# Delta net's merges: the 64 by 64 products of two heads staggered instead of all eight at once

## The chip, the cores and the metric

The kernel runs on one core of a Trainium2 chip. The metric is the device time of one execution in microseconds (us); the time of a kernel is the median of its runs. Before the change that is 2497.89 us, the median of three runs from 2497.13 to 2501.19 us.

Engines are named as the profile names them: PE is TensorE's matmul and PEld its weight load, DVE is VectorE, ACT is ScalarE, POOL is GpSimd and SP is the engine that issues most of the DMAs.

## The reference, cut to what matters

The program is a small streaming encoder on 1024 tokens of width 1024: one gated DeltaNet layer with a gated ConvFFN, then one chunked attention layer with another ConvFFN, then a norm. The change lies in the DeltaNet layer. There, for each of 8 heads and each chunk, a unit lower triangular matrix is solved against the values and the keys:

```python
m = jnp.where(strict, jnp.einsum("bhnid,bhnjd->bhnij", k_beta, k) * decay, 0.0)
eye = jnp.eye(CHUNK, dtype=m.dtype)
rhs = jnp.concatenate([v * beta[..., None], k_beta * jnp.exp(gcum)[..., None]], axis=-1)
uw = lax.linalg.triangular_solve(m + eye, rhs, left_side=True, lower=True, unit_diagonal=True)
```

After it a scan over the chunks carries a 128 by 128 state per head.

## The kernel before, in words

**The stage.** The kernel works on chunks of 128 tokens, so there are 8 chunks, and each of the 8 heads has a 128 by 128 triangular matrix per chunk. Heads and chunks are cut in four groups `t`: group `t` holds four heads (0 to 3 or 4 to 7) and four chunks (`s`, the first or the second half of the sequence). For each group the steps are: `gram` (products of keys, one matrix `mn` per chunk), `invert_blocks` (inverts the 16 by 16 blocks on the diagonal), `merge` twice (`j` = 0, 1; each for two heads with four chunks each, so eight matrices), `prep`, `chain` (the scan, per head four chunks of small fp32 matmuls at lines 926, 930 and 939), `output` and `finish`. That makes eight merges.

**A merge** puts the inverse `U` of a 128 by 128 matrix together from the inverted blocks: first 16 by 16 blocks into 32 by 32 (lines 845 and 851), then those into 64 by 64 (lines 862, 872 and 874), then those into 128 by 128. The last doubling has two products of 64 by 64 for each of the eight matrices. The lower half, line 881, reads rows 0 to 63 of `mn` and of `TY` and writes rows 64 to 127 of `pm`, a tile in PSUM. ACT copies that into `TY[64:128]` (line 883). The corner, line 886, reads rows 64 to 127 of `TY` and of `U` and writes rows 0 to 63 of `pm`, and ACT copies it into `U` (line 888). `pm` is one tile of 128 rows by 8 matrices by 64 columns, with one buffer, and all the products of a merge write into it, lines 845 to 874 too. Products in fp32 are run as two passes, so eight products are 16 matmul instructions in the trace.

**What sets the order.** While these small steps run, PE works through the dense projections: matmuls of 128 by 128 weights with 512 columns, three per step (lines 118, 119 and 120, split precision; `acc` for the input projections, `acco` for the output projection). The order of PE's, DVE's and ACT's instructions is written out when the program is built, by a planner, the class `Flow`. It keeps a clock `T` of PE and a free time for each other engine. Each step of the small work is a generator that says what it costs (`wv.pe(n, dt)` moves `T`, `wv.on("A", cost)` books time on ACT) and yields the time at which its results should be there; `run` takes the first small step whose time has come (plus a slack of 0.5), and else one dense step. A step's `wv.mark(("merged", hd, s), t)` lets that head's `chain` start; the marks of all heads let the output projection start, through `begin`. So a step that is cut in two, or another cost or yield, moves other steps in the program as well, though it adds no instruction to them.

Of the kernel before, what the change touches and what calls it, by code (L numbers as in the profile page):

```python
# [28 lines left out]
def trunk_kernel(  # L29
# [15 lines left out]
    nc = tc.nc  # L45
# [32 lines left out]
    mm = nc.tensor.matmul  # L78
# [321 lines left out]
    wv = None  # L400
# [107 lines left out]
    with ExitStack() as ph:  # L508
# [137 lines left out]
        def heads(t):  # L646

            return t // 2, range(4 * (t % 2), 4 * (t % 2) + 4)
# [172 lines left out]
        TY = dq.tile([P, 8, 64], F32, name="TY")  # L821
        nc.gpsimd.memset(TY, 0.0)

        def merge(t, j):

            b = [slice(32 * i, 32 * i + 32) for i in range(4)]
            D = dq.tile([P, 8, 32], F32, name="D", tag="D", bufs=1)
            s, hds = heads(t)
            hds = hds[2 * j : 2 * j + 2]
            for a in range(2):  # L830
                nc.sync.dma_start(out=D[:, 4 * a : 4 * a + 4], in_=d_us[t][2 * j + a].rearrange("c b j i -> (b j) c i"))
            U = dp.tile([P, 8, P], F32, name="U", tag="U", bufs=2)
            nc.gpsimd.memset(U, 0.0)
            wv.on("G", 0.83)
            yield wv.T + 4.5 - wv.slack
            T = dq.tile([P, 8, 32], F32, name="T", tag="T", bufs=1)
            X = dq.tile([P, 8, 32], F32, name="X", tag="X", bufs=1)
            pm = pone.tile([P, 8, 64], F32, name="pm", tag="pm")
            blocks = [(a, c, 4 * a + c) for a in range(2) for c in range(4)]
            mn = [mns[hd, s] for hd in hds]  # L840
            nc.vector.transpose(T.rearrange("p c i -> p (c i)"), D.rearrange("p c i -> p (c i)"))
            yield wv.on("D", 0.5)
            for a, c, n in blocks:
                for i in range(4):
                    mm(pm[b[i], n, 0:32], mn[a][b[i], c, b[i]], T[b[i], n], start=True, stop=True)
            wv.pe(32, 0.03)
            nc.scalar.copy(X, pm[:, :, 0:32])
            yield wv.on("A", 0.39)
            for a, c, n in blocks:
                for i in range(4):  # L850
                    mm(pm[b[i], n, 32:64], X[b[i], n], D[b[i], n], start=True, stop=True)
            wv.pe(32, 0.03)
            nc.vector.scalar_tensor_tensor(D[:, :, 16:32], pm[:, :, 48:64], upper, D[:, :, 16:32], op0=ALU.mult, op1=ALU.add)
            nc.vector.transpose(T.rearrange("p c i -> p (c i)"), D.rearrange("p c i -> p (c i)"))
            t_ = wv.on("D", 0.85)
            for i in range(4):
                nc.gpsimd.tensor_copy(U[b[i], :, b[i]], D[b[i]])
            wv.on("G", 1.37, t_)
            yield t_
            for a, c, n in blocks:  # L860
                for i in (0, 2):
                    mm(pm[b[i + 1], n, 0:32], mn[a][b[i], c, b[i + 1]], T[b[i], n], start=True, stop=True)
            wv.pe(16, 0.04)
            for i in (1, 3):
                nc.scalar.copy(X[b[i]], pm[b[i], :, 0:32])
            t_ = wv.on("A", 0.74)
            for i in (0, 1):
                nc.scalar.copy(TY[b[i], :, b[i]], T[b[i]])
            wv.on("A", 0.8)
            yield t_  # L870
            for a, c, n in blocks:
                mm(pm[b[1], n, 32:64], D[b[1], n], X[b[1], n], start=True, stop=True)
                for i in (0, 2):
                    mm(pm[b[i], n, 32:64], X[b[i + 1], n], D[b[i + 1], n], start=True, stop=True)
            wv.pe(24, 0.04)
            nc.scalar.copy(TY[b[1], :, 0:32], pm[b[1], :, 32:64])
            for i in (0, 2):
                nc.vector.tensor_copy(U[b[i], :, b[i + 1]], pm[b[i], :, 32:64])
            yield max(wv.on("D", 0.8), wv.on("A", 0.4))
            for a, c, n in blocks:  # L880
                mm(pm[64:128, n], mn[a][0:64, c, 64:128], TY[0:64, n], start=True, stop=True)
            wv.pe(8, 0.12)
            nc.scalar.copy(TY[64:128], pm[64:128])
            yield wv.on("A", 0.6)
            for a, c, n in blocks:
                mm(pm[0:64, n], TY[64:128, n], U[64:128, n, 64:128], start=True, stop=True)
            wv.pe(8, 0.12)
            nc.scalar.copy(U[0:64, :, 64:128], pm[0:64])
            t_ = wv.on("A", 0.6)
            for a, hd in enumerate(hds):  # L890
                Us[hd, s] = U[:, 4 * a : 4 * a + 4]
                wv.mark(("merged", hd, s), t_)

        outs = [-1, -1]
        states = dp.tile([P, 8, P], F32, name="states")
# [339 lines left out]
        kqs, mns, parts, Us = {}, {}, {}, {}  # L1235
# [94 lines left out]
        wv = Flow()  # L1330
# [20 lines left out]
        with tc.manual_schedule(engines={mybir.EngineType.PE, mybir.EngineType.DVE, mybir.EngineType.Activation}):  # L1351
# [4 lines left out]
            for t in range(4):  # L1356
                s, hds = heads(t)
                for hd in hds:
                    wv.add(2, "sq", wv.when(("q", hd, 0) if s == 0 else ("in", hd)), qnorm(hd, s))
                    if s == 1:  # L1360
                        wv.add(1, "fetch", wv.when(("out", hd, 0), ("k", hd, 1), ("q", hd, 1)), fetch_kq(hd))
                wv.add(2, "gram", wv.when("gates"), gram(t))
                wv.add(2, "solve", wv.when(*[("gram", hd, s) for hd in hds]), invert_blocks(t))
                for j in range(2):
                    free = [("chain", t - 1, j)] if t > 0 else []
                    for hd in hds[2 * j : 2 * j + 2]:
                        wv.add(3, "prep", wv.when(("v", hd, s), ("qn", hd, s), ("scale", t), ("gram", hd, s), *free), prep(hd, s))
                        wv.add(0, ("chain", hd % 2), lambda: 0.0, chain(t, hd))
                    wv.add(1, "merge", wv.when(("solved", t), *free), merge(t, j))
                    wv.add(2.5, ("joined", t, j), lambda: 0.0, joined(t, j))  # L1370
                    wv.add(2, "finish", wv.when(("chain", t, j), *[("qn", hd, s) for hd in hds]), finish(t, j))
# [725 lines left out]
    with ExitStack() as ph:  # L2097
# [17 lines left out]
        wv = Flow()  # L2115
# [300 lines left out]
        def close(p, a, tp, oT, t):  # L2416
            if p == 7 and a == 1 and tp % 2 == 1:
                wv.add(1, ("own", tp // 2), wv.when(("acts", tp // 2)), own_act(oT, tp // 2, 7))
            if p < 7 and (a, tp) == (1, 3):
                if p == 6:  # L2420
                    for s in range(2):
                        wv.add(2, ("own", s), wv.when(("acts", s)), own_act(oT, s, 6))
                wv.mark(("o", p), t)
                if p < 6:
                    wv.later(t + 5.0, lambda: (nc.sync.dma_start(out=d_o[p], in_=oT), wv.mark(("d_o", p), wv.T + 5.31)))

        def own_act(oT, s, k):
            split_act(acts, oT[:, hs(s)], s, k)
            t = wv.on("A", 0.31)
            wv.mark(("act", k, s), wv.on("D", 1.09, t) if k % 2 == 0 else wv.on("G", 2.22, t))  # L2430
            return
            yield
# [291 lines left out]
```

## Time and profile before

| what | value |
|---|---|
| runs | 2497.13, 2497.89, 2501.19 us; median 2497.89 |
| profiled execution, first to last instruction (its own time) | 2493.3 us |
| PE busy | 2466.1 us, 99%, 13785 matmuls |
| DVE, ACT, POOL busy | 1842.5, 1442.1, 1523.0 us (74%, 58%, 61%) |
| TensorE clock granted | 9 tenths or more in every slice |
| merges | from 152.3 us (first product of the first) to about 541 us (last product of the eighth) |

A row of the profile that names a line stands for all instructions of that line on one engine: their count, the time in which at least one ran, the mean duration of one, and the idle time of the engine ahead of them with what ended it. Matmuls overlap: a dense matmul of 512 columns shows a duration of about 390 ns though the next starts 230 ns later. So what a piece of PE's work costs is read from starts, from the first instruction of the piece to the first one behind it.

### The profile page before, as it was taken

What the parts mean: (1) busy time and instruction counts of PE and PEld (TensorE: products, weight loads), DVE (VectorE), ACT (ScalarE), POOL (GpSimd) and SP (SyncE); (2) the same over time, 40 slices, a digit from 0 to 9 for tenths busy, and PEclk for the clock granted to TensorE, in tenths of its full rate; (3) what the DMA queues carried; (4) which work ended last, traced back from release to release, by engine and by line L of the source; (5) the groups of instructions that cost most, each with busy time, mean ns of one, the idle gap of its engine ahead of it and who ended that gap; (6) DMA issues with size and microseconds to landing.
All of it is one profiled execution on the core that took longest, in us unless ns stands there. A gap on an engine that the chain in (4) does not pass through costs nothing.

```text
span 2493.3 us, 39279 instructions
## 1 busy us (share of the span) xinstructions
PE 2466.1 (99%) x13785; PEld 2057.0 (83%) x13785; DVE 1842.5 (74%) x2985; ACT 1442.1 (58%) x2770; POOL 1523.0 (61%) x1548
## 2 busy tenths in 40 slices
PE   8999999999999999999999999999999999999998
PEld 6888888888888888888788888888877888888877
DVE  5665874567798888888866656666589788888886
ACT  6444546474465556565555666667456565666555
POOL 3655653357357777777626454455554777778774
PEclk9999999999999999999999999999999999999999
DMA  8734435565347777777841232333444799777788
GB/s 228 188 105 118 142 110 153 156 194 163 96 108 148 150 153 151 153 144 156 183 151 55 67 80 77 81 76 95 145 114 119 184 176 180 166 169 171 152 187 224
DMA packets 383877, 353.19 MB, mean 142 GB/s; under 512 B 97600, under 2 KB 304448, under 8 KB 383680
## 3 DMA queue, kind: packets, MB, share of 16 engines
q1 hardware_dynamic: 350704, 243.46, 34.4%
q0 software_dynamic: 28224, 98.58, 22.5%
q10 hardware_dynamic: 4752, 8.65, 0.9%
q8 instruction: 108, 1.77, 0.3%
q14 instruction: 89, 0.73, 0.1%
HBM read 182.25 MB, written 156.30 MB: 136 GB/s over the span
## 4 chain that ended last, share of the span: by engine, by line
PE 81%; POOL 6%; DVE 4%; issue 4%; DMA 2%; ACT 2%; SPq 0%; ACTq 0%; POOLq 0%; DVEq 0%
PE acc L118 8%; PE pu L1448 8%; PE acc L119 8%; PE acc L120 8%; PE pu L1446 8%; PE pu L1447 8%; PE pd L1448 3%; PE pd L1446 3%; PE pd L1447 3%; POOL ul L1412 3%; PE acco L118 2%; PE acco L120 2%; PE acco L119 2%; PE ptp L2353 2%; PE poT L2399 1%
## 5 line engine op out<-in xcount | busy, mean ns | idle before, releaser
L1412 POOL TENSOR_TENSOR ul<-r,uh 128x512 fp32r<-128x512 f32 x266 | 430.4, 1638 | 258.3 <-ACT uh L1434 253.5
L118 PE MATMUL acc<-xh,whi 128*128 128x512 f32 x896 | 369.3, 413 | 0.5 <-ACT xh L1094 0.5
L119 PE MATMUL acc<-xl,whi 128*128 128x512 f32 x896 | 352.1, 393 | 0.4 <-POOL xl L381 0.3
L120 PE MATMUL acc<-xh,wlo 128*128 128x512 f32 x896 | 351.3, 392 | 0.0
L103 POOL TENSOR_TENSOR wlo<-wraw,whi 128x256 fp32r<-128x256 f32 (+1 forms) x326 | 237.0, 758 | 107.8 <-ACT whi L101 105.3
L1434 ACT CAST uh<-r 128x512 fp32r<-128x512 f32 x289 | 177.1, 623 | 183.3 <-DVE r L1412 148.8
L1448 PE MATMUL pu<-xh,ul 128*128 128x512 f32 x524 | 204.4, 390 | 0.7 <-POOL ul L1412 0.7
L1446 PE MATMUL pu<-xh,uh 128*128 128x512 f32 x524 | 204.4, 390 | 0.7 <-ACT keep L1575 0.7
L1802 ACT COPY stage<-pd 128x1024 f32<-128x1024 f32 x180 | 175.3, 1014 | 49.7 <-PE pd L1448 48.8
L1447 PE MATMUL pu<-xl,uh 128*128 128x512 f32 x524 | 203.9, 389 | 0.0
L120 PEld LDWEIGHTS acc<-xh,wlo 128*128 128x128 f32 x896 | 168.5, 188 | 37.1
L2308 POOL TENSOR_SCALAR sS<-sS,st 128x640 f32<-128x640 f32 (+4 forms) x128 | 87.6, 691 | 178.4 <-DVE st L2306 168.2
L119 PEld LDWEIGHTS acc<-xl,whi 128*128 128x128 f32 x896 | 169.3, 189 | 28.4 <-POOL xl L381 2.5
L118 PEld LDWEIGHTS acc<-xh,whi 128*128 128x128 f32 x896 | 169.1, 189 | 27.5 <-ACT xh L1094 0.9
L1412 POOL TENSOR_TENSOR dl<-a,dh 128x512 fp32r<-128x512 f32 x90 | 153.3, 1703 | 47.4 <-ACT dh L1434 37.2
L1541 DVE SCALAR_TENSOR_TENSOR gate<-gpre,colt,gate 128x1023 f32<-128x1023 f32 (+2 forms) x92 | 176.5, 1919 | 2.5 <-ACT gate L1538 1.8
L1541 DVE SCALAR_TENSOR_TENSOR val<-vpre,colt,val 128x1023 f32<-128x1023 f32 x88 | 149.2, 1696 | 29.3 <-ACT val L1538 29.3
L2298 DVE CUSTOM_DVE_ANT_0 sS<-sc,bt 128x640 f32<-128x640 f32 (+4 forms) x128 | 84.1, 657 | 111.4 <-PE sc L2294 75.9
L1412 DVE TENSOR_TENSOR r<-r,r 128x512 f32<-128x512 f32 x160 | 130.3, 814 | 32.8 <-POOL ul L1412 31.7
L1412 DVE TENSOR_TENSOR el<-val,eh 128x512 fp32r<-128x512 f32 x90 | 85.4, 949 | 43.2 <-ACT eh L1434 43.2
L1448 PEld LDWEIGHTS pu<-xh,ul 128*128 128x128 f32 x524 | 98.4, 188 | 22.8 <-POOL ul L1412 1.4
L1446 PEld LDWEIGHTS pu<-xh,uh 128*128 128x128 f32 x524 | 98.4, 188 | 21.1 <-ACT keep L1575 1.1
(428 smaller groups left out, 7197.9 us busy)
## 6 DMA issues: line engine op xcount, KB each, us to landing
r<-in_f_w_up_dram SPq DMA_DIRECT2D x176, 256.0 KB, 4.5
d_r<-stage POOLq DMA_DIRECT2D x78, 512.0 KB, 8.1
d_c<-stage POOLq DMA_DIRECT2D x70, 512.0 KB, 8.4
a<-in_f_w_down_dram SPq DMA_DIRECT2D x72, 256.0 KB, 2.9
wraw<-in_a_w_in_dram SPq DMA_DIRECT2D x32, 512.0 KB, 4.5
d_e<-stage POOLq DMA_DIRECT2D x32, 512.0 KB, 8.3
wraw<-in_a_w_out_dram SPq DMA_DIRECT2D x16, 512.0 KB, 4.1
d_r<-h ACTq DMA_DIRECT2D x32, 256.0 KB, 2.8
```

Of the source, the lines that this page charges most:

```text
L103: nc.gpsimd.tensor_tensor(lo[:, c], raw[:, c], hi[:, c].bitcast(F32), op=ALU.subtract)
L118: mm(ps, hi[:, kw, wcol : wcol + P], rh[k][s], start=st, stop=False)
L119: mm(ps, hi[:, kw, wcol : wcol + P], rl[k][s], start=False, stop=False)
L120: mm(ps, lo[:, kw, wcol : wcol + P], rh[k][s], start=False, stop=sp)
L1412: tt = lambda eng, o, a, b, op: eng.tensor_tensor(o, a, b, op=op)
L1434: copy(hi, src)
L1446: mm(ps, w[0][:, cw], x[0], start=first, stop=False, skip_group_check=True)
L1447: mm(ps, w[0][:, cw], x[1], start=False, stop=False, skip_group_check=True)
L1448: mm(ps, w[1][:, cw], x[0], start=False, stop=last, skip_group_check=True)
L1541: nc.vector.scalar_tensor_tensor(t_[:, a:c1], p_[:, a - step : c1 - step], w[:, 2 - step : 3 - step], t_[:, a:c1], op0=ALU.mult, op1=ALU.add)
L1802: nc.scalar.copy(t_, ps)
L2308: nc.gpsimd.tensor_scalar(S, S, st[:, 3:4], 1.0, op0=ALU.mult, op1=ALU.mult)
```

## The change

The eight lower halves and the eight corners of a merge are no longer two blocks of eight. The four lower halves of the first head run alone. Then the four corners of the first head run in turns with the four lower halves of the second head. Then the four corners of the second head run alone. The copies of ACT are cut by head: two into `TY` and two into `U` in place of one each. The first head is marked as merged after the middle block, the second after the last. The planner is told other costs (`wv.pe(4, 0.12)`, `wv.pe(4, 0.14)`, `wv.pe(4, 0.12)` and four copies of 0.4 in place of two of 0.6), and there is one more yield.

```diff
-            for a, c, n in blocks:
-                mm(pm[64:128, n], mn[a][0:64, c, 64:128], TY[0:64, n], start=True, stop=True)
-            wv.pe(8, 0.12)
-            nc.scalar.copy(TY[64:128], pm[64:128])
-            yield wv.on("A", 0.6)
-            for a, c, n in blocks:
-                mm(pm[0:64, n], TY[64:128, n], U[64:128, n, 64:128], start=True, stop=True)
-            wv.pe(8, 0.12)
-            nc.scalar.copy(U[0:64, :, 64:128], pm[0:64])
-            t_ = wv.on("A", 0.6)
-            for a, hd in enumerate(hds):
-                Us[hd, s] = U[:, 4 * a : 4 * a + 4]
-                wv.mark(("merged", hd, s), t_)
+            def low(a, c):
+                mm(pm[64:128, 4 * a + c], mn[a][0:64, c, 64:128], TY[0:64, 4 * a + c], start=True, stop=True)
+
+            def corner(a, c):
+                mm(pm[0:64, 4 * a + c], TY[64:128, 4 * a + c], U[64:128, 4 * a + c, 64:128], start=True, stop=True)
+
+            def close(a):
+                nc.scalar.copy(U[0:64, 4 * a : 4 * a + 4, 64:128], pm[0:64, 4 * a : 4 * a + 4])
+                Us[hds[a], s] = U[:, 4 * a : 4 * a + 4]
+                wv.mark(("merged", hds[a], s), wv.on("A", 0.4))
+
+            for c in range(4):
+                low(0, c)
+            wv.pe(4, 0.12)
+            nc.scalar.copy(TY[64:128, 0:4], pm[64:128, 0:4])
+            yield wv.on("A", 0.4)
+            for c in range(4):
+                corner(0, c)
+                low(1, c)
+            wv.pe(4, 0.14)
+            nc.scalar.copy(TY[64:128, 4:8], pm[64:128, 4:8])
+            t_ = wv.on("A", 0.4)
+            close(0)
+            yield t_
+            for c in range(4):
+                corner(1, c)
+            wv.pe(4, 0.12)
+            close(1)
```

In the changed kernel the lower half keeps line 881, the corner is line 884, the copies are lines 894 and 900 (`TY`) and 887 (`U`), and every later line stands 15 further down. The number of instructions is the same on PE, DVE, POOL and SP; ACT has 16 copies more.

On PE, in the first merge, before the change (`pk` are transposes for `prep`, `acc` is the dense work):

```order
L881 MATMUL pm<-TY,mn 64x64 x8
L750 MATMUL pk<-ident,kq 128x128 x4
L118 MATMUL acc<-xh_0_247,whi 128x512
L119 MATMUL acc<-xl_0_248,whi 128x512
L120 MATMUL acc<-xh_0_247,wlo 128x512
L118 MATMUL acc<-xh_0_251,whi 128x512
L119 MATMUL acc<-xl_0_252,whi 128x512
L120 MATMUL acc<-xh_0_251,wlo 128x512
L886 MATMUL pm<-U,TY 64x64 x8
```

The same place of PE after the change:

```order
L881 MATMUL pm<-TY,mn 64x64 x4
L750 MATMUL pk<-ident,kq 128x128 x4
L118 MATMUL acc<-xh_0_247,whi 128x512
L119 MATMUL acc<-xl_0_248,whi 128x512
L120 MATMUL acc<-xh_0_247,wlo 128x512
L118 MATMUL acc<-xh_0_251,whi 128x512
L119 MATMUL acc<-xl_0_252,whi 128x512
L120 MATMUL acc<-xh_0_251,wlo 128x512
L884 MATMUL pm<-U,TY 64x64
L881 MATMUL pm<-TY,mn 64x64
L884 MATMUL pm<-U,TY 64x64
L881 MATMUL pm<-TY,mn 64x64
```

The block of lower halves has become four, and the block of corners a mix of four and four (the rest of it goes on in the same way); the last four corners come as a third block after four more dense steps.

On ACT, at the same merge, before the change, from the copy into `TY` to the one into `U`:

```order
L883 COPY TY<-pm 64x512
L754 ACTIVATE ke<-pk,ekd 128x128 x4
L625 ACTIVATE th<-u 128x512
L101 CAST whi<-wraw 128x1024
L888 COPY U<-pm 64x8x64
```

And after the change:

```order
L894 COPY TY<-pm 64x256
L754 ACTIVATE ke<-pk,ekd 128x128 x4
L101 CAST whi<-wraw 128x1024
L625 ACTIVATE th<-u 128x512
L900 COPY TY<-pm 64x256
L887 COPY U<-pm 64x4x64
```

The copy that the last four corners wait for, line 900, stands behind the same four `ke`, one cast of weights and one `th`.

On PE, at the end of the eighth merge, where the dense work of the input projections runs out and the output projection (`acco`) begins, before the change (`pc` is the chain):

```order
L886 MATMUL pm<-U,TY 64x64 x8
L118 MATMUL acc<-xh_1_261,whi 128x512
L119 MATMUL acc<-xl_1_262,whi 128x512
L120 MATMUL acc<-xh_1_261,wlo 128x512
L930 MATMUL pc<-vv,U 128x128 x2
L118 MATMUL acco<-xh_0_6121,whi 128x512
```

And after the change (`pv` are transposes for `prep`; lines 941 and 945 are what lines 926 and 930 were):

```order
L118 MATMUL acc<-xh_1_261,whi 128x512
L119 MATMUL acc<-xl_1_262,whi 128x512
L120 MATMUL acc<-xh_1_261,wlo 128x512
L945 MATMUL pc<-vv,U 128x128
L941 MATMUL pc<-states,kq 128x128
L884 MATMUL pm<-U,TY 64x64 x4
L778 MATMUL pv<-ident,vv 128x128 x4
L945 MATMUL pc<-vv,U 128x128
L118 MATMUL acco<-xh_0_6146,whi 128x512
```

The last block of corners now stands behind the last dense step of the input projections, and between that step and the first one of the output projection there are five pieces of small work instead of one.

## The prediction, on record before the result

> **What bounds the kernel now.** I read the page first, for the engine that has no room.
>
> ```profile
> span 2493.3 us, 39279 instructions
> PE 2466.1 (99%) x13785; PEld 2057.0 (83%) x13785; DVE 1842.5 (74%) x2985; ACT 1442.1 (58%) x2770; POOL 1523.0 (61%) x1548
> ```
>
> PE is busy for 99% of the span. That is an average over very different stages, so next comes the stretch in which the eight merges lie, by the view of windows and by the view of waits with PE as the one that waits.
>
> ```profile
> 150.00:550.00 400.00, 399.56 (x3948) 340.19 (x3947) 244.13 (x689) 219.70 (x637) 198.89 (x268) 1.00 0.48 142
> PE po L985 <- DVE mn L724: 0.2, 1, 0.2
> PE pv L778 <- DMA vv<-d_v: 0.2, 1, 0.2
> ```
>
> The columns of the first line are the stretch, its length, and the busy time of PE, PEld, DVE, ACT and POOL; then the clock and the DMA share. Of 400 us PE has 399.56 busy, and it waited twice, 0.2 us each, neither time in a merge. DVE, ACT and POOL have at least 155 us free each. So in this stage a microsecond is won only by giving PE less to do, or lost by giving it more or by making it wait. What the groups of lines say of the two products and of the copies behind them is the same:
>
> ```profile
> L881 PE MATMUL pm<-TY,mn 64*64 64x64 f32 x128 | 9.1, 221 | 0.0
> L886 PE MATMUL pm<-U,TY 64*64 64x64 f32 x128 | 9.1, 221 | 0.0
> L883 ACT COPY TY<-pm 64x512 f32<-64x512 f32 x8 | 4.7, 582 | 14.0 <-PE pm L881 14.0
> L888 ACT COPY U<-pm 64x512 f32<-64x512 f32 x8 | 4.6, 580 | 10.3 <-PE pm L886 10.3
> ```
>
> PE has no idle time ahead of either product; ACT waits for PE, 14.0 and 10.3 us in all, and not the other way round. The latency of a merge (products, copy, products, copy) is covered by dense work. All that the change can touch directly is 9.1 + 9.1 = 18.2 us of PE's time, 0.7% of the span.
>
> **The change part by part.**
>
> *A block of eight products.* The timeline of PE around the corners of the first merge (start, duration, engine and line; x16 because a product is two passes):
>
> ```profile
> 166.01 0.40 PE L119 MATMUL acc<-xl,whi 128*128 128x512 f32 x1
> 166.24 0.40 PE L120 MATMUL acc<-xh,wlo 128*128 128x512 f32 x1
> 166.57 1.14 PE L886 MATMUL pm<-U,TY 64*64 64x64 f32 x16
> 167.64 0.50 PE L118 MATMUL acc<-xh,whi 128*128 128x512 f32 x1
> 167.98 0.39 PE L119 MATMUL acc<-xl,whi 128*128 128x512 f32 x1
> 168.21 0.40 PE L120 MATMUL acc<-xh,wlo 128*128 128x512 f32 x1
> ```
>
> From start to start a dense matmul takes 166.24 - 166.01 = 0.23 us. Into the block it is 166.57 - 166.24 = 0.33, so the entry costs 0.10; the block lasts 167.64 - 166.57 = 1.07; and the first dense step behind it takes 167.98 - 167.64 = 0.34, 0.11 too much. A block of eight costs 1.07 + 0.21 = 1.28 us, of which 0.21 are paid for being a block at all. Two blocks per merge make 2.56 us.
>
> *A block of four.* A window cut through the block of lower halves of the first merge, and the whole block, tell the price of a pass:
>
> ```profile
> 163.51 0.62 PE L881 MATMUL pm<-TY,mn 64*64 64x64 f32 x7
> 163.51 1.14 PE L881 MATMUL pm<-TY,mn 64*64 64x64 f32 x16
> ```
>
> Nine passes more take 1.14 - 0.62 = 0.52 us, 0.058 each. Four products are eight passes fewer: 1.07 - 8 x 0.058 = 0.61, and with entry and exit 0.82 us. Two such blocks per merge: 1.64 us.
>
> *The mixed block.* Corners read rows 64 to 127 and write rows 0 to 63, lower halves the other way, so they use different rows and different columns of the array. No row shows two tiles of 64 by 64 at once. The nearest rows are the merge's own products of 32 by 32, line 845 on four tiles and line 862 on two (row strips 0 and 2), which write into the same `pm`:
>
> ```profile
> 152.28 0.75 PE L845 MATMUL pm<-T,mn 32*32 32x32 f32 x64
> 152.97 0.50 PE L118 MATMUL acc<-xh,whi 128*128 128x512 f32 x1
> 157.74 0.69 PE L862 MATMUL pm<-T,mn 32*32 32x32 f32 x32
> 158.36 0.50 PE L118 MATMUL acc<-xh,whi 128*128 128x512 f32 x1
> ```
>
> From start to the next start 64 passes take 152.97 - 152.28 = 0.69 us and 32 passes take 158.36 - 157.74 = 0.62. Both have 16 passes on each tile that they use. So the time goes by the passes on one tile, and tiles with rows and columns of their own run side by side. The mixed block has 16 passes, eight on each of two tiles, and by that row should last as long as eight on one: 0.61, plus about 0.02 until the second tile starts (line 845's two more tiles cost 0.07), plus 0.21: 0.84 us.
>
> *Sum for a merge:* 0.82 + 0.84 + 0.82 = 2.48 against 2.56, 0.08 us less; eight merges, 0.6 us less. The gain is so small because the overlap saves 1.07 - 0.63 = 0.44 us, but a third block pays 0.21 outside and, beyond its passes, 0.61 - 8 x 0.058 = 0.15 inside. The bounds: if the two tiles take turns, the mixed block costs 1.28, the merge 2.92, and eight merges are 2.9 us slower. If the third block had its entry and exit for nothing, the gain would be 0.6 + 8 x 0.21 = 2.3 us. I take the middle value, since rows of the same merge show the overlap and each block quoted here pays to enter and to leave.
>
> On the overlap, the Trainium skill, "TensorEngine Tiling (Array Packing)", Gotcha 1, says that different row tiles cannot access the same PSUM bank at the same time; all eight matrices of `pm` lie in one tile of PSUM, so by that rule the mixed block would take turns and the sum would be the slower bound. Line 862, with two row strips in the same `pm`, runs as fast per tile as line 845 with four, which speaks against it here; but no run here shows it for 64 by 64.
>
> *The moved order.* The planner sets many small steps elsewhere. In the built programs the dense work between the first product of keys and the ConvFFN stands in 181 unbroken stretches before and 213 after; 30 of the 32 new breaks are single pieces of the chain. What such a break costs:
>
> ```profile
> 521.56 0.39 PE L119 MATMUL acc<-xl,whi 128*128 128x512 f32 x1
> 521.79 0.39 PE L120 MATMUL acc<-xh,wlo 128*128 128x512 f32 x1
> 522.02 0.61 PE L930 MATMUL pc<-vv,U 128*128 128x128 f32 x4
> 522.38 0.48 PE L118 MATMUL acc<-xh,whi 128*128 128x512 f32 x1
> 522.70 0.39 PE L119 MATMUL acc<-xl,whi 128*128 128x512 f32 x1
> ```
>
> Entry 522.02 - 521.79 = 0.23, as between dense ones; the piece 0.36; the dense step behind it 0.32 instead of 0.23. That is 0.36 + 0.09 = 0.45 us for four passes of 128 columns, about 0.11 each, and these passes stand in the program either way. 30 breaks at 0.00 to 0.02 us are 0 to 0.6 us; I take 0.
>
> *ACT, the waits and the queues.* ACT's 16 copies become 32. A copy of 256 columns takes 0.364 us:
>
> ```profile
> L876 ACT COPY TY<-pm 32x256 f32<-32x256 f32 x8 | 2.9, 364 | 3.0 <-PE pm L874 2.9
> L101 ACT CAST whi<-wraw 128x1024 fp32r<-128x1024 f32 x23 | 24.0, 1045 | 0.0
> 164.69 0.58 ACT L883 COPY TY<-pm 64x512 f32<-64x512 f32 x1 [2.95 <-PE pm L881]
> 165.30 1.15 ACT L754 ACTIVATE ke<-pk,ekd 128x128 f32<-128x128 f32 x4
> 166.32 0.65 ACT L625 ACTIVATE th<-u 128x512 f32<-128x512 f32 x1
> ```
>
> Four of them less one each of lines 883 and 888 are 1.46 - 1.16 = 0.30 us per merge, 2.4 us in all, under 180 us in which ACT is free: nothing. The new wait is the third block's, for line 900. Queued behind it on PE are the dense steps and the chain, so a late copy stops everything. In the first merge line 900 stands behind `ke` (1.15), a cast (1.05) and a `th` (0.65). These begin while the dense steps ahead of the mixed block still run, and behind it PE has four dense steps, 12 x 0.23 = 2.8 us, before it needs the copy. Covered; uncovered it would cost at most the cast, about 1 us in one merge. No DMA is added; POOL's and SP's instructions keep their number, and their places move with the planner's clock, as DVE's do. `U` of the second head is complete a block later, and its chain begins later by some dense steps; nothing on PE stands idle for that as long as dense work is left.
>
> *The sum* against the profiled execution: 2493.3 - 0.6 = 2492.7 us. The median of the runs is 2497.89 - 2493.3 = 4.6 us above that span, which I carry over: 2497.3 us.
>
> **The rivals.** About 0.2%, 5 us, is what a measurement of this kernel can tell from no change; the three runs before lie 4.1 us apart.
>
> *Turns (0.12).* The two tiles of the mixed block don't overlap: 2497.89 + 2.9 = 2500.8 us, slower than before, and it decides as soon as the mixed block lasts more than 0.63 + 0.08 = 0.71 us, for then the third block is no longer earned. For it speaks that no row has 64 by 64 tiles at once; against it line 862.
>
> *A drain at each change of tile (0.03).* If each of the 7 changes between corner and lower half cost what entering a block does, 0.10 us, on top of taking turns, a merge would be 0.36 + 0.7 = 1.06 us longer and the kernel 8.5 us: 2506.4 us, the one case beyond what a measurement can miss. Line 845 changes its tile with each product and has no room for such a price: 64 passes in 0.69 us. The same page of the Trainium skill, Tiling Modes, says that a change of mode drains the array and a mere change of tile does not, which line 845 bears out.
>
> *Starving at the hand-over (0.12).* At the end of the eighth merge the last corners now stand behind the last dense step of the input projections, with five small pieces up to the first `acco`. There no dense work is left to cover a late copy, a late `vv` for the transposes, or the chain's step on DVE. The waits seen in the stage are 0.2 us; an uncovered copy and cast are 1.4 us, and two such waits 2.8 us: 2497.3 + 2.8 = 2500.1 us. For it speaks the order; against it that PE reached `acco` without idle time before, and runs a little behind whatever it waits for.
>
> *A better order (0.03).* Both 0.2 us waits go and the third block enters beside other small work: down to 2497.89 - 2.3 - 0.4 = 2495.2 us.
>
> That the change doesn't do what it says is no case of its own: the order shows the mixed block in the merges.
>
> **How the numbers follow.** My forecast, overlap and no new wait, has 0.70: 2497.3 us. The range has to hold the better order (2495.2) and turns (2500.8), and a median of three runs that lie 4 us apart adds some 1 us at each end: 2494.0 to 2501.8 us; the drain and mishaps at several places stay outside. Within 0.2% are the forecast, turns, starving and most of the better order; slower by more has the drain and a part of starving; faster by more would need a gain that no row here offers: 0.02, 0.92, 0.06.
>
> **What would show it.** In the profile after: blocks of line 881 with x8 lasting 0.61 from start to the next start; a mixed block near 0.63 (right) or 1.07 (turns) or 1.77 (drain); a dense step behind each block of 0.34; PE's waits between 150 and 550 us still under 1 us in all, and none ahead of `acco`. The forecast is wrong if the time leaves 2494 to 2501.8 us, or if PE shows a wait of a microsecond or more in this stage.

## The result, and the profile after

The change makes the kernel slower. The median of 5 runs is 2508.45 us (2505.39 to 2510.12), that of 5 runs of the kernel before beside them 2497.42 us (2494.95 to 2501.19). The ratio is 1.0034, 95% interval 1.0023 to 1.0046. The same program in a second series (e4, below) took 2506.96 us against 2498.58, ratio 1.0032 [1.0022, 1.0042]. So the change costs 8 to 11 us, where 0.6 us less was forecast; 2508.45 us lies outside the range of 2494.0 to 2501.8.

The page of the profile after:

```profile
span 2506.9 us, 39305 instructions
PE 2470.8 (99%) x13785; PEld 2056.4 (82%) x13785; DVE 1843.1 (74%) x2985; ACT 1445.8 (58%) x2786; POOL 1522.8 (61%) x1548
```

The span is 2506.9 - 2493.3 = 13.6 us longer. That is more than the change costs, because the execution profiled before was a quick one: a run's time is 1.7 us above the span of the same execution (2508.60 for this span of 2506.9), so that execution took about 2495.0 us, 2.4 under the median of 2497.42. PE does the same 13785 matmuls, is busy 4.7 us longer, and stands idle for 2506.9 - 2470.8 = 36.1 us where it stood idle for 27.2: 8.9 us more. DVE, ACT and POOL have no more work than before, but for ACT's 16 copies. So the loss is waits of PE, and dense steps that took longer.

First the blocks, since the prediction rests on them. PE's timeline of the first merge after the change, around the mixed block and the last corners:

```profile
166.51 0.40 PE L120 MATMUL acc<-xh,wlo 128*128 128x512 f32 x1
166.84 0.27 PE L884 MATMUL pm<-U,TY 64*64 64x64 f32 x1
166.84 0.27 PE L881 MATMUL pm<-TY,mn 64*64 64x64 f32 x1
166.94 0.22 PE L884 MATMUL pm<-U,TY 64*64 64x64 f32 x1
166.95 0.22 PE L881 MATMUL pm<-TY,mn 64*64 64x64 f32 x1
...
167.29 0.22 PE L884 MATMUL pm<-U,TY 64*64 64x64 f32 x1
167.30 0.22 PE L881 MATMUL pm<-TY,mn 64*64 64x64 f32 x1
167.45 0.50 PE L118 MATMUL acc<-xh,whi 128*128 128x512 f32 x1
167.79 0.39 PE L119 MATMUL acc<-xl,whi 128*128 128x512 f32 x1
...
170.41 0.68 PE L884 MATMUL pm<-U,TY 64*64 64x64 f32 x8
171.02 0.50 PE L118 MATMUL acc<-xh,whi 128*128 128x512 f32 x1
```

Each corner starts in the same hundredth or one ahead of the lower half beside it, so the two tiles run side by side. The mixed block of 16 passes lasts 167.45 - 166.84 = 0.61 us, as long as a block of eight passes on one tile, 171.02 - 170.41 = 0.61. It is the same in all eight merges: each of the 24 blocks lasts 0.60 or 0.61 us, 14.58 us together, where the 16 blocks of before lasted 17.15. The groups of the two lines, for the stretch from 150 to 550 us:

```profile
L881 PE MATMUL pm<-TY,mn 64*64 64x64 f32 x128 | 10.8, 224 | 0.0
L884 PE MATMUL pm<-U,TY 64*64 64x64 f32 x128 | 10.8, 224 | 0.0
```

There is no idle time ahead of either, as before. (Their busy time is 10.8 where it was 9.1, since the two lines now run at the same time and each is counted; what they cost PE is read from starts.) What changed is who waits elsewhere. The view of waits, PE as the one that waits, from 150 to 625 us:

```profile
PE pc L945 <- DVE vv L943: 2.5, 3, 1.1
PE pm L862 <- issue: 1.8, 1, 1.8
PE pq L655 <- DMA kq<-d_kq: 0.9, 1, 0.9
PE pm L845 <- DVE T L841: 0.9, 1, 0.9
PE pc L954 <- ACT y L950: 0.4, 1, 0.4
PE pc L941 <- DVE S L960: 0.2, 1, 0.2
```

Before, this list held the two waits of 0.2 us that the prediction quotes and nothing else. After, it holds 4.9 us of waits for other engines and a stop of 1.8 us named "issue". None of the lines is one that the change edits: 945, 941 and 954 are the chain, 655 transposes, 845 the start of a later merge. The stretch from 500 to 550 us, before and then after (columns as in the prediction's windows):

```profile
500.00:550.00 50.00, 50.00 (x714) 42.86 (x714) 30.25 (x64) 36.80 (x94) 24.83 (x29) 1.00 0.65 199
```

```profile
500.00:550.00 50.00, 47.38 (x577) 39.69 (x578) 25.07 (x57) 33.49 (x89) 20.65 (x24) 0.97 0.59 183
```

PE has 2.6 us idle where it had none, and the granted clock is 0.97. (The counts of matmuls, 714 and 577, are not a loss by themselves: the program has moved by some microseconds by then, so the two windows hold different pieces.) A second place lies far behind the last merge, at the hand-over to the ConvFFN: from 620 to 700 us the clock is 0.98 where it was 1.00. It is taken up below, under the wait for memory.

**A wait of the new order, in its place.** PE and DVE around 564 us, after the change (line 943 makes the `vv` that line 945 needs; lines 542 to 547 are the small steps of `finish`):

```profile
562.77 0.40 PE L120 MATMUL acco<-xh,wlo 128*128 128x512 f32 x1
564.24 0.49 PE L945 MATMUL pc<-vv,U 128*128 128x128 f32 x2 [1.07 <-DVE vv L943]
```

```profile
559.76 0.58 DVE L984 SCALAR_TENSOR_TENSOR ff<-gg,ff 128x8 f32<-128x8 f32 x1
...
563.42 0.17 DVE L547 SCALAR_TENSOR_TENSOR rr<-t,rr 128x8 f32<-128x8 f32 x1
563.50 0.45 DVE L1314 COPY xs<-xm 128x512 uint16<-128x512 uint16 x1
563.84 0.34 DVE L943 SCALAR_TENSOR_TENSOR vv<-pc,neg_eg,vv 128x128 f32<-128x128 f32 x1
```

DVE is busy without a break from 558.43 on, and the chain's step stands behind all of `finish` and a copy. Before, the same kind of step (line 928) stood ahead of those small steps, at 554.05, and PE did not wait. Nothing was added; two queues were only put in another order. This wait stands among dense steps, and so do others: the one at 487.65 us has dense steps of the input projections directly ahead of it and directly behind. Dense work that is written behind a waiting matmul waits with it.

**A wait for memory.** The ConvFFN's weight loads (`r`) are issued by SP one behind the other. The first two are issued at once; the rest start late. SP's timeline before, then after:

```profile
640.81 10.79 SPq L1492 DMA_DIRECT2D r<-in_f_w_up_dram  x10
```

```profile
655.51 7.19 SPq L1507 DMA_DIRECT2D r<-in_f_w_up_dram  x10
```

What released them, by the time, is a step of DVE, 0.03 us earlier in both: line 359 before, line 364 after, each the one that reads a square `sq` for the norm.

```profile
639.01 1.77 DVE L359 TENSOR_TENSOR run<-run,sq 128x512 f32<-128x512 f32 x1
```

```profile
654.79 0.69 DVE L364 TENSOR_TENSOR nacc<-run,sq 128x512 f32<-128x512 f32 x1 [0.47 <-ACT sq L357]
```

In the built programs that load's buffer covers the first of the three buffers of tag `zt`, which the squares take in turns with other tiles of the stage (`th`, `zt`, `yo`). Which buffer the last square gets depends on how often the ring has turned by then, so on the order. Before, the last square lies in the third buffer, and the load waits for an earlier square. After, the last square lies in the first, and the load waits for the very end of the layer. What that costs, on ACT and PE:

```profile
658.55 0.62 ACT L1449 CAST uh<-r 128x512 fp32r<-128x512 f32 x1 [3.78 <-DMA r<-in_f_w_up_dram]
```

```profile
659.22 0.50 PE L1461 MATMUL pu<-xh,uh 128*128 128x512 f32 x1 [1.82 <-ACT uh L1449]
...
659.94 0.80 PE L1463 MATMUL pu<-xh,ul 128*128 128x512 f32 x1
660.54 1.91 PE L385 MATMUL psb<-ident,rsn 128*128 128x128 f32 x8
```

ACT waits 3.78 us for the load, PE 1.82 us for ACT, and then PE is slow: the granted clock is 0.50 for 3.41 us, from 659.83 us on, a dense matmul shows 0.80 instead of 0.39 us, and line 385's block shows 1.91 where it shows 1.05 in a kernel without that wait (e3).

### The profile page after: what moved, and what is told of

Its sections match the earlier page's. It is cut to its first block, busy times and chain, and to the rows that moved or that the text cites. A ratio compares the mean times of both kernels' runs of the same rounds, so it can differ in the third digit from the quotient of the medians.

```text
span 2506.9 us, 39305 instructions
## 1 busy us (share of the span) xinstructions
PE 2470.8 (99%) x13785; PEld 2056.4 (82%) x13785; DVE 1843.1 (74%) x2985; ACT 1445.8 (58%) x2786; POOL 1522.8 (61%) x1548
## 3 DMA queue, kind: packets, MB, share of 16 engines
q8 instruction: 108, 1.77, 0.3%
## 4 chain that ended last, share of the span: by engine, by line
PE 79%; POOL 6%; DVE 5%; issue 4%; DMA 3%; ACT 2%; SPq 0%; ACTq 0%; POOLq 0%; DVEq 0%
PE pu L1463 8%; PE pu L1461 8%; PE acc L118 8%; PE pu L1462 8%; PE acc L119 8%; PE acc L120 8%; PE pd L1462 3%; PE pd L1461 3%; PE pd L1463 3%; POOL ul L1427 3%; PE ptp L2368 2%; PE acco L118 2%; PE acco L120 2%; PE acco L119 2%; PE poT L2414 1%
```

## The experiments

Three theories were set against each other. Theory 1, the order: the edit's costs and yields shift the planner, and the waits come from the shifted order, whatever the products do. Theory 2, the products: running them in turns, with three blocks in place of two, costs more than starts show. Theory 3, the reused memory, is a part of the first with a place of its own: the load that waits for the last square. The ratios below are each against the kernel before on the same chip (2498.43 to 2498.70 us).

**e1, the new order without the turns.** The changed kernel, but all eight lower halves stand together again, with one copy behind them; the rest of the order is that of the change.

```diff
-            for c in range(4):
-                low(0, c)
+            for h_ in range(2):
+                for c in range(4):
+                    low(h_, c)
             wv.pe(4, 0.12)
-            nc.scalar.copy(TY[64:128, 0:4], pm[64:128, 0:4])
+            nc.scalar.copy(TY[64:128], pm[64:128])
...
-                low(1, c)
-            nc.scalar.copy(TY[64:128, 4:8], pm[64:128, 4:8])
```

> The order of every instruction of PE, DVE and ACT is that of the changed kernel, and the planner is told the same numbers; only the products stand otherwise: all eight lower halves in the first block, the first head's corners alone in the second, the second head's alone in the third, so no two tiles ever run side by side. Theory 1 (the loss is in the new order of the other work; the products in turns gain a little): the loss stays, and the blocks cost 1.28 + 0.82 + 0.82 = 2.92 us per merge instead of the 2.48 of the changed kernel, 3.5 us more in all: 2508.5 + 3.5 = about 2512 us, with the same waits of PE at the same places. Theory 2 (the products in turns are what costs): without them the time goes back to the old one plus the third block, 2497.4 + 8 x 0.36 = about 2500 us.

Measured: 2514.66 us (2512.12 to 2520.22), ratio 1.0062 [1.0048, 1.0076]. It is slower still, as theory 1 has it, and by more than it expected. Its waits:

```profile
PE pq L655 <- DMA kq<-d_kq: 3.4, 2, 2.6
PE pm L862 <- issue: 1.9, 1, 1.9
PE pc L944 <- DVE vv L942: 1.7, 3, 0.7
PE pm L845 <- DVE T L841: 0.9, 1, 0.9
PE pc L940 <- DVE S L959: 0.8, 1, 0.8
```

Four of the five are waits of the change, with other sizes, and the wait for the load of `kq` is 2.5 us longer. The loss doesn't need the turns. The blocks did cost 3.7 us more than in the change (18.26 us against 14.58), close to the 3.5 forecast; the longer wait for `kq`, with the clock at 0.50 for 3.41 us from 433.84 us on, was not forecast.

**e2, the turns in the old order.** The planner gets the costs, yields and marks of before; the products are staggered as in the change, and the last corners are put behind the third dense step that follows.

```diff
+            def third():
+                for c in range(4):
+                    corner(1, c)
+                close(1)
...
-            wv.pe(4, 0.14)
+            wv.pe(8, 0.12)
...
+            wv.third = [3, hds[1], third]
+            t_ = wv.on("A", 0.6)
+            for a, hd in enumerate(hds):
+                Us[hd, s] = U[:, 4 * a : 4 * a + 4]
+                wv.mark(("merged", hd, s), t_)
```

> The products in three blocks as in the changed kernel, with the copies cut by head, but the planner is told the numbers of the kernel before and has its two steps; the third block is put in three dense steps later without the planner's knowledge. PE's, DVE's and ACT's other instructions stand in the order of the kernel before. Theory 1 (the new order costs): the loss is gone and the predicted 0.6 us are gained, 2497.4 - 0.6 = about 2496.8 us, with PE's waits between 150 and 650 us under 2 us. Theory 2 (the products in turns or the third block's copy cost): about 2508 us, with waits of PE ahead of the corners.

Measured: 2499.56 us (2492.94 to 2504.30, 11 runs), ratio 1.0000 [0.9992, 1.0009]. With the products in turns and the old order the loss is gone. Theory 2 falls, within the interval of some 2 us to each side. In the profile PE has no idle time ahead of the corners, and its waits for others from 150 to 650 us are 1.6 us, under the 2 us forecast; a stop of 2.3 us named "issue", in a block of line 873 (line 862 of before), comes on top of them. The 0.6 us that the blocks save lie within the interval, so they are neither shown nor excluded.

**e3, the last square moved.** The changed kernel, with the last square of the layer in a free buffer of the late `xs` tiles, which no weight load reuses.

```diff
-            sq = acc if k == 0 else env["tmp"]()
+            sq = acc if k == 0 else env["end"]() if run is not None and s == 1 and k == KT - 1 else env["tmp"]()
...
+        env["end"] = lambda: late.tile([P, HALF], F32, name="sqe", tag="xs", bufs=2)
```

> The changed kernel, with the last square of the first ConvFFN's norm put into a buffer of the residual (xs) instead of the ring of three that squares, gates and outputs share; no instruction is added or moved. Theory 3 (half of the loss is at the entry of the ConvFFN: the second weight load, queued first in line on SP, now lands in the memory of that last square and waits for the end of the norm, and ACT and PE wait for the load): the load of the second weight tile goes out some 10 us earlier relative to the norm, PE's wait of 1.8 us for ACT near 659 us and the slow clock behind it are gone, 4 to 5 us less: about 2504 us. If the place of the buffer does not matter: 2508.5 us.

Measured: 2504.09 us (2502.76 to 2506.14, 11 runs), ratio 1.0020 [1.0011, 1.0028]. That is 4.4 us under 2508.45, and 2.9 under the second series of the change (e4), which ran beside it on the same chip. So the 2504 that was expected was met in part by luck: against its own series the move is worth less than the 4 to 5 us forecast. ACT at the same place:

```profile
655.51 0.62 ACT L1450 CAST uh<-r 128x512 fp32r<-128x512 f32 x1 [0.47 <-DMA r<-in_f_w_up_dram]
```

The wait of 3.78 us is 0.47, PE waits for no `uh` there, and the clock from 620 to 700 us is 1.00 again. So theory 3 explains somewhat over a third of the loss (2.9 of 8.4, 4.4 of 11.0). The rest, 5 us, is still there, and so are the waits from 150 to 625 us:

```profile
...
PE pc L945 <- DVE vv L943: 1.5, 3, 0.6
PE pq L655 <- ACT junk L978: 1.1, 1, 1.1
PE pq L655 <- DMA kq<-d_kq: 0.9, 1, 0.9
PE pm L845 <- DVE T L841: 0.9, 1, 0.9
PE pc L941 <- DVE S L960: 0.9, 1, 0.9
...
```

They come to 5.3 us; left out are one of 0.2 us (line 120, for POOL) and the stop named "issue", 1.6 us here.

**e4, the change once more,** with no edit, for a second profile.

> The changed kernel once more, unchanged, for a second profile: which of PE's new waits belong to the program and which to the one execution. The waits for DVE near 311, 488, 540 and 564 us, and the one at the entry of the ConvFFN, follow from the order and from the buffers and should be there again within 0.3 us; the stop of 1.8 us within the products of line 862 near 504 us, for which the trace names no engine, is open: there again if it belongs to a place in the program, gone if it was chance. Time about 2508 us.

Measured: 2506.96 us (2503.99 to 2508.59, 8 runs), ratio 1.0032 [1.0022, 1.0042]. Its profiled execution has the same waits (2.6 for line 945, 0.9, 0.9, 0.5), but the stop named "issue" is 0.6 us instead of 1.8, and its span is 2502.3 us, 4.6 less than that of the first profile. A profile of one execution is not a measurement of the difference.

**e5 and e6, one number of the planner.** The kernel before, products and copies untouched; only the slack is another.

```diff
-        wv.slack = 0.5
+        wv.slack = 0.45
```

> The kernel before, its products untouched, with one number of the planner changed: slack 0.45 instead of 0.5, which puts the small steps elsewhere among the dense ones. The ring of three buffers comes out as in the changed kernel (the last square of the norm in the memory of the second weight tile). Theory 1 with theory 3 (any new order brings waits of some microseconds, and this ring costs 4 to 5 at the entry of the ConvFFN): 2503 to 2509 us, with a wait of PE of about 1.8 us for ACT at the ConvFFN's first products. If the loss belonged to the staggered products: 2498.6 us, as before.

> The kernel before with slack 0.55; the order moves as well, but the ring comes out as in the kernel before. Theory 3: no wait at the entry of the ConvFFN. Theory 1: new waits in the stage of 0 to 6 us: 2498 to 2505 us; if the order of the kernel before were nothing special, about as many waits as there, 2498.6 us.

Measured: 2509.01 us (2506.36 to 2515.45), ratio 1.0044 [1.0031, 1.0056], for 0.45; 2501.63 us (2499.20 to 2503.80, 11 runs), ratio 1.0011 [1.0002, 1.0020], for 0.55. With 0.55 the time is as expected; with 0.45 it is at the upper edge of what was expected. A number that changes no instruction can cost as much as the whole change. In the stage from 150 to 625 us PE's waits for others are 2.8 us with 0.45, besides a stop "issue" of 1.4, and 4.3 us with 0.55. With 0.45 the last square lies in the first buffer, as after the change, and PE waits 1.9 us for `uh`; with 0.55 it lies in the third and there is no such wait.

**e7, the change with the slack at 0.55.**

```diff
-        wv.slack = 0.5
+        wv.slack = 0.55
```

> The changed kernel with slack 0.55. The ring comes out a third way: the last square but one lies in the memory of the second weight tile. Theory 3: that load waits for a step some 5 us earlier than in the changed kernel, so the 4 to 5 us at the entry go; theory 1: the waits in the stage come out another way, 0 to 6 us. Together 2498 to 2505 us. If the staggered products cost the time: 2508 us whatever the order.

Measured: 2509.07 us (2507.18 to 2513.39), ratio 1.0044 [1.0032, 1.0056]. This is a miss. The last square lies in the second buffer and PE's wait for `uh` is down to 0.8 us, as theory 3 has it; but this order has larger waits in the stage:

```profile
PE pm L845 <- DVE T L841: 3.9, 2, 2.9
PE pc L945 <- DVE vv L943: 3.0, 2, 2.3
PE pc L941 <- DVE S L960: 0.9, 2, 0.7
PE acc L118 <- DVE u L620: 0.6, 1, 0.6
```

8.4 us in all. Theory 1 says that a new order has other waits; it can't say which without the program having run.

**e8, 64 instructions more ahead.** The first merge repeats four of its 32 by 32 products, which writes the same values again. It was to show whether the stop in line 862 goes by the place in the stream of instructions.

```diff
-            for a, c, n in blocks:
+            for a, c, n in (blocks[0:4] if t + j == 0 else []) + blocks:
```

> The changed kernel with half of the first products of line 845 in the first merge done twice (same values into the same place): 32 passes, 64 instructions more on PE (a weight load and a matmul each), about 0.35 us, and nothing else moved. For the stop within line 862 near 504 us. In all the profiles so far such a stop stands at PE instruction 8129 or 8897, and 8897 - 8129 = 768 = 3 x 256. If it is the fetch of the next 256 instructions, all places move by 64: the stop is no longer within line 862 but 64 instructions earlier in the program, within line 851, or it is gone because that place is reached at another time. If it belongs to line 862 (its data, its tiles), it stays there. Time 2508 us, less up to 3 us if the stop is gone.

Measured: 2506.57 us (2503.67 to 2511.68), ratio 1.0033 [1.0022, 1.0045]. In the one profile there is no stop in line 862; two waits of line 655 are longer or new (2.0 us for the DMA of `kq`, 1.4 for ACT). The execution without the stop took 2508.26 us, as long as the change, so the stop is not what makes the change slower. Where the stop comes from this run alone doesn't decide, since other profiles have none either; the last section takes it up.

**e9 to e11, the last square moved in three other kernels.** The edit is that of e3: in the kernel before with slack 0.45 (e5), in the kernel before itself, and in e2.

> The kernel before with the planner's slack at 0.45 (products and copies untouched; it took 2509.0 us against 2498.4) and the last square of the layer in the free buffer of the late xs tiles. Theory of the reused memory: the ConvFFN's second weight load no longer stands behind the square, ACT's wait for it before the first gate activation (3.9 us) and PE's wait of 1.9 us for that go, and the time falls by 3 to 4.5 us, to about 2505; what is left above 2498.4 are the waits of the shifted order. If the memory is not the cause in this order: 2509, unchanged.

> The kernel before with nothing but the last square of the layer moved to the free buffer. There the square already lies in a buffer that the weight load does not reuse, and no wait for that load is seen. Theory of the reused memory: no change, 2498.4 +- 1.5 us. If the move is a gain of its own in any order (an earlier load, less on DVE's queue): about 2495.

> The products in turns, put into the order of the kernel before (2499.6 us against 2498.6 without the move), and the last square moved. The candidate for the best of both: the blocks save 0.6 us, no wait of the new order, no wait for the weight load. 2498 us, from 2496.5 to 2499.5, which cannot be told from before; by the theory that the overlap of the products is worth more once nothing else disturbs, 2495 or less.

Measured: e9 2503.59 us (2502.20 to 2512.39), ratio 1.0021 [1.0012, 1.0031]; e10 2498.36 us (2495.87 to 2501.76), 0.9998 [0.9990, 1.0007]; e11 2499.85 us (2494.84 to 2504.01), 0.9999 [0.9990, 1.0007]. In e9 the move is worth 2509.01 - 2503.59 = 5.4 us, a little more than the 3 to 4.5 expected, though its ten runs fall into six from 2502.20 to 2503.68 and four from 2506.76 to 2512.39; in e10, where no wait was to be removed, nothing. That is theory 3 in a program with the products of before. e11 was to beat both kernels and doesn't: no version here is measurably faster than the kernel before.

e10 showed something else as well. It has the order of before on PE until the ConvFFN. The block of line 862 near 530 us, in the kernel before and then in e10:

```profile
529.95 0.72 PE L862 MATMUL pm<-T,mn 32*32 32x32 f32 x32
```

```profile
530.81 0.37 PE L862 MATMUL pm<-T,mn 32*32 32x32 f32 x10
533.71 0.78 PE L862 MATMUL pm<-T,mn 32*32 32x32 f32 x22 [2.53 <-issue]
```

The same instructions in the same order run through in one execution and stop for 2.53 us in the other. e10's span is 2496.8 us, and 2496.8 - 2.5 = 2494.3 is near the 2493.3 of before. So whether PE stops there belongs to the execution. The profile from which the prediction was made is one without it. Of the 4.6 us from that span to the median, 1.7 lie between the span and the time of every run, and the other 2.9 are a quick execution.

## Why the prediction was wrong, point by point

*A block of four, 0.61 us, and entry and exit 0.21.* Right: 0.61 from start to the next start; the dense step behind takes 171.35 - 171.02 = 0.33 where 0.34 was forecast.

*The mixed block, 0.63 us, two tiles side by side.* Right, 0.61. The rival of turns (1.07) and that of a drain at each change of tile (1.77) are out. The Trainium skill, "TensorEngine Tiling (Array Packing)", Gotcha 1, says that different row tiles can't use the same PSUM bank at once. Here that cost no time: the two tiles use rows 0 to 63 and 64 to 127 of the array, write the same tile `pm`, start within 0.01 us of each other, and 16 passes last as long as eight.

*ACT's copies cost nothing.* Right: no idle time of PE ahead of lines 881 and 884.

*The sum, 0.6 us less.* By the starts it is there: inside the blocks PE spends 17.15 - 14.58 = 2.57 us less, and eight more blocks pay at most 8 x 0.21 = 1.7 us to enter and to leave. e2 shows that it can't be measured, with an interval of about 2 us to each side.

*"30 breaks at 0.00 to 0.02 us are 0 to 0.6 us; I take 0."* This is the step that failed. It priced a moved piece by how long the piece takes at its new place. The cost is not there: it is in who is not ready at the new place. The prediction saw 32 new breaks, and that DVE's and POOL's places move too, and then treated each queue as if it moved alone. Its reason, that "nothing on PE stands idle for that as long as dense work is left", is what the traces contradict: the waits at 310.72 and 487.65 us have dense steps directly ahead of them and behind. What the runs showed instead: 4.9 us of waits from 150 to 625 us after the change against 0.4 before, no loss when the order of before is kept with the new products (e2), and the same kind of loss from the slack alone (e5).

*Starving at the hand-over (0.12, two waits of 1.4 us).* The mechanism was right in kind and wrong in place and size. It named one place, the end of the eighth merge. A wait of 0.87 us for the chain's DVE step does stand there, at 540.47 us. Others for that step stand at 487.65 and 564.24 us, one for a DVE step of a merge at 310.72, and one for the load of `kq` at 429.55. The range left "mishaps at several places" outside; the result lies there.

*A part that the prediction didn't have:* it read the profile to 550 us, since the merges end there. The order also decides which buffer the last square gets, and by that when the ConvFFN's weights can be loaded, 100 us later. By e3 and e9 this is 2.9 to 5.4 us.

*The base, 4.6 us from the span to the median.* Carrying it over was right: the programs that keep the old order (e2, e10, e11) come out at the median of before. It holds 1.7 us that every run has and 2.9 us by which the profiled execution was quicker than the median.

How far the parts add up: e3 against e10, both with the square moved, is 2504.09 - 2498.36 = 5.7 us. In e3's profile the waits for others from 150 to 625 us are 5.3 + 0.2 = 5.5 us, in e10's 0.6; with 0.6 saved by the blocks that makes 4.3. The remaining 1.4 us are open, and single executions can't settle them: e3's profile has a stop "issue" of 1.6 us, e10's one of 2.53 us and 3.41 us at half the clock behind it. The waits were read from profiles and not taken away one by one; that the order as a whole causes them is shown by e1, e2 and e5.

## What to carry to other kernels

When a planner writes out the order, an edit to its costs is an edit to the whole program: before taking 0 for the moved steps, compare in the built program, for each waiting instruction of the engine that has no room, what now stands ahead of its producer on the producer's queue, and which buffers are reused by whom. A small gain in such a kernel is best tried in the old order (as in e2), and the spread between orders is measured by turning one number that changes no instruction (as in e5 and e6): here that alone moved the time by 3 to 11 us, far more than the gain that was looked for. And look behind the stage that is edited: a ring of buffers carries a change of order to the next one.

## What the runs showed of the hardware

**The clock after a short stop.** The windows from 620 to 665 us, before and after:

```profile
620.00:665.00 45.00, 44.44 (x204) 36.48 (x203) 29.41 (x41) 20.14 (x33) 25.61 (x28) 1.00 0.51 149
```

```profile
620.00:665.00 45.00, 42.20 (x181) 33.46 (x180) 25.65 (x35) 16.48 (x25) 29.85 (x34) 0.96 0.55 168
```

Behind the wait of 1.82 us the granted clock falls to 0.50 for 3.41 us, and matmuls in that time show about twice their duration. By estimate, from these two numbers, that costs 3.41 x 0.5 = 1.7 us of PE's work on top of the wait. After their first 20 us the thirteen profiles hold 19 idle times of PE over 1.3 us. At the end of 13 of them, from 1.37 (e5) to 2.89 us (e7), the clock went to 0.50 for 3.41 us (6.83 once, in e5), at the earliest 0.8 us before PE went on and at the latest 1.8 us behind. With the other six it stayed at 1.00: 1.32 (e9), 1.33 (e5), 1.40 (e8), 1.60 (e3), 2.00 (e8) and 2.34 us (e7). So the length alone does not decide. The Trainium skill, "TensorE: Matmul & The Clock Gate", Why this matters for your kernels, advises no idle gaps over about 3 us. Here shorter ones were enough in two cases of three, so a wait of 2 us can cost nearly twice its own length.

**A stop that comes and goes.** In nine of the thirteen profiles PE stopped once inside a block of line 862 (873 in e2 and e11), with no engine and no load of the kernel to wait for: 0.6 and 1.8 us in two executions of the change, 0 and 2.53 us in two with the order of before. Its place is one of two in the stream of PE's matmuls and weight loads, 768 of them apart (in e5 and e9 six further on). The pages list a DMA queue for instructions, first that of the change, then that of e8, which has 64 instructions more on PE (packets, MB, share of the 16 DMA engines):

```profile
q8 instruction: 108, 1.77, 0.3%
```

```profile
q8 instruction: 109, 1.79, 0.3%
```

108 packets (of 16384 bytes) for PE's 2 x 13785 = 27570 matmuls and weight loads are 255 for each packet, and 768 are three times 256, so the packets look like PE's own instructions. In all nine profiles PE goes on 1.3 to 1.5 us after one of them has landed: the 31st of the run in the six with a moved order, the 34th in the three with the order of before (e2, e10, e11), three packets apart like the two places. In e10 the 34th was sent at 531.49 us and had landed at 532.43; PE went on at 533.71. In the kernel before it was sent at 527.58 and had landed at 528.62; PE came to that place at 530.12, 1.50 us later, and did not stop. So what PE stopped for was, by these times, its next instructions, which were sent later and not more slowly (0.95 us against 1.04). No run moved such a packet, and why it is sent later in some executions is open.
